# Storing one head's last rows through GpSimd in 17 small DMAs

## The chip, the cores and the metric

The kernel runs on one core of a Trainium2 chip. The core has a matrix engine (TensorE, in the profile PE, its weight loads PEld), VectorE (DVE), ScalarE (ACT), GpSimd (POOL) and SyncE (SP, which here only issues DMAs), and 16 DMA engines that move data between HBM and the on-chip memory SBUF. The results of TensorE land in PSUM and have to be copied to SBUF before a DMA can take them. The metric is the device time of one execution in microseconds (us). Before the change it is 1063.38 us, the median of 3 runs (1062.9 to 1063.62).

## The reference

For each of 8 x 12 = 96 heads, q and k are 1024 x 64 matrices in float32, and the output is the 1024 x 1024 matrix of their dot products:

```python
def reference(q, k):                      # q, k: (8, 12, 1024, 64) float32
    return np.einsum('bhid,bhjd->bhij', q, k).astype(np.float32)
```

The inputs are 50.3 MB together, the output is 402.7 MB: 4 MB (4096 KB) for each head.

## The kernel before

The 96 heads are worked off in blocks of 2, 2, 4, 8, 8 and then six times 12 heads (`sizes`). For each block, q and k are loaded in float32, cast to fp16 by GpSimd (`cast_rows`, `cast_quads`), and transposed, by TensorE for the two small blocks at the start and by VectorE for the others (`transpose_rows`, `transpose_quads`), so that the 64 elements of a row lie along partitions. Loads, casts and transposes of a later block run beside the scores of the present one. GpSimd's last cast ends long before the kernel does; after it GpSimd has nothing to do.

`scores(n, ...)` computes one head. Its output tile `o_sb` is 128 partitions x 8 rows x 1024 floats: partition p holds the output rows 8p to 8p+7, 32 KB in all, which lie side by side in HBM too. The head goes in four pieces (`u`), each of two rows of each partition: four matmuls into a PSUM tile (L171), then one copy PSUM to SBUF by ScalarE (L181), 128 x 2048 floats. After the fourth copy SP issues one DMA (L185) that stores the whole 4096 KB of the head. There are 96 such stores, all in SP's queue. SP waits before each for ScalarE's last copy of that head.

`out_pool` has three buffers, so ScalarE's first copy of head n waits until the store of head n-3 has landed. The program ends when the last store, that of head 95, has landed (SP waits for it at L304) and all engines have met in a barrier.

Instructions are issued in the order in which the source writes them (`pin` is `tc.keep_in_program_order`). The head that the change is about is `BH - 2`, number 94 counted from 0, the last but one. Its buffer isn't used again, since only head 95 comes after it, which takes the buffer of head 92.

Of the kernel before, what the change touches and what calls it, by code (L numbers as in the profile page):

```python
# [10 lines left out]
P = 128  # L11

@with_exitstack
def kernel(
# [6 lines left out]
    nc = tc.nc  # L21

    B, H, S, D = q.shape
    NT = S // P
    BH = B * H
# [5 lines left out]
    of = out.rearrange("b h i j -> (b h) i j")  # L31
# [4 lines left out]
    NMAX = max(sizes)  # L36
    CHUNK = 48 * 32

    consts = ctx.enter_context(tc.tile_pool(name="consts", bufs=1))
    ident = consts.tile([P, P], F16)  # L40

# [3 lines left out]
    out_pool = ctx.enter_context(tc.tile_pool(name="out_pool", bufs=3))  # L45

    pin = tc.keep_in_program_order

    def half_tile():
        half_sb = half_pool.tile([P, CHUNK], F16, tag="half")  # L50
        return half_sb

    class Block:
# [102 lines left out]
        def scores(self, n, side, ps_pool, w):  # L156

            half, g = divmod(n, self.N // 2)
            cs = slice(half * D, (half + 1) * D)

            qT = self.qT.rearrange("c (g m t) -> c g t m", t=NT, m=P)
            kT = self.kT.rearrange("c (g j) -> c g j", j=S)
            o_sb = out_pool.tile([P, NT, S], F32, tag="out")
            for u in range(NT // w):
                ps = ps_pool.tile([P, w * S], F32, tag="po")
                for tt in range(w):
                    for j in range(2):
                        js = slice(j * 512, (j + 1) * 512)
                        at = tt * S + j * 512
                        pin(  # L170
                            nc.tensor.matmul(  # L171
                                ps[:, at : at + 512],
                                qT[cs, g, w * u + tt],
                                kT[cs, g, js],
                            )
                        )
                dst = o_sb[:, w * u : w * u + w].rearrange("p t j -> p (t j)")
                if w == 1 and u % 2:
                    pin(nc.vector.tensor_copy(out=dst, in_=ps))  # L179
                else:  # L180
                    pin(nc.scalar.copy(out=dst, in_=ps))  # L181
                for do in side.get(u, []):
                    do()
            pin(
                nc.sync.dma_start(  # L185
                    out=of[self.first + n].rearrange("(p t) j -> p (t j)", p=P),
                    in_=o_sb.rearrange("p t j -> p (t j)"),
                )
            )

    blocks, first = [], 0
    for i, N in enumerate(sizes):
# [116 lines left out]
```

## Time and profile before

| | |
|---|---|
| median of 3 runs | 1063.38 us (1062.9 to 1063.62) |
| profiled execution: span from the first to the last instruction, the only time that its page gives | 1061.8 us |
| median less that span | 1.6 us |
| DMA traffic | 453.25 MB, mean 427 GB/s |
| busy share of PE / ACT / DVE / POOL | 66% / 66% / 44% / 35% |
| SP's stores | 96 of 4096 KB, median 21.8 us from issue to landing |
| last two stores issued by SP | about 1030.0 and 1039.4 us |
| GpSimd's last cast ends | 832.1 us |

The profile page gives the busy share of each engine, of the 16 DMA engines together, and the rate at which they move bytes, in 40 slices of the span. Views of the trace give the same for any stretch, the waits of each engine by what ended them, and the chain of work that ended last. In the view of stretches, a DMA packet (one partition's run of bytes) is counted in the stretch in which it starts, so a share over short stretches can exceed 1 or fall to 0 while an engine is still at work on one packet.

### The profile page before, as it was taken

What the parts mean: (1) busy time and instruction counts of PE and PEld (TensorE: products, weight loads), DVE (VectorE), ACT (ScalarE), POOL (GpSimd) and SP (SyncE); (2) the same over time, 40 slices, a digit from 0 to 9 for tenths busy, and PEclk for the clock granted to TensorE, in tenths of its full rate; (3) what the DMA queues carried; (4) which work ended last, traced back from release to release, by engine and by line L of the source; (5) the groups of instructions that cost most, each with busy time, mean ns of one, the idle gap of its engine ahead of it and who ended that gap; (6) DMA issues with size and microseconds to landing.
All of it is one profiled execution on the core that took longest, in us unless ns stands there. A gap on an engine that the chain in (4) does not pass through costs nothing.

```text
span 1061.8 us, 4282 instructions
## 1 busy us (share of the span) xinstructions
PE 701.3 (66%) x1568; PEld 241.6 (23%) x1568; DVE 471.5 (44%) x75; ACT 697.6 (66%) x386; POOL 368.3 (35%) x286
## 2 busy tenths in 40 slices
PE   6866755755677367773677836777367777778770
PEld 2322211211222122221222212222122222222220
DVE  2999601991696007960079600795007950000000
ACT  4856745755777366774677746777467777777771
POOL 6959128607630463303733046330463200000000
DMA  9999999999999999999999999999999999999997
GB/s 385 428 429 435 433 431 435 435 422 440 428 430 432 432 430 432 435 422 429 431 433 431 415 436 431 433 435 422 428 434 435 434 432 432 434 433 427 434 431 311
DMA packets 17588, 453.25 MB, mean 427 GB/s; under 512 B 1952, under 2 KB 1952, under 8 KB 2976
## 3 DMA queue, kind: packets, MB, share of 16 engines
q1 hardware_dynamic: 14688, 406.85, 89.1%
q10 hardware_dynamic: 2880, 46.14, 10.4%
q8 instruction: 12, 0.20, 0.1%
q14 instruction: 8, 0.07, 0.0%
HBM read 50.33 MB, written 402.65 MB: 427 GB/s over the span
## 4 chain that ended last, share of the span: by engine, by line
DMA 70%; ACT 17%; PE 7%; DVE 2%; issue 1%; POOL 1%; ACTq 0%; SPq 0%
DMA out_dram<-o_sb 70%; ACT o_sb L181 17%; PE ps L171 7%; DVE qT L145 1%; DVE kT L145 1%; DMA early<-in_q_dram 0%; POOL half_sb L127 0%; PE ps L151 0%; POOL half_sb L97 0%; DVE kT L154 0%; DVE o_sb L179 0%; ACTq L181 0%; ACT kT L154 0%; SPq L84 0%; ACTq L73 0%
## 5 line engine op out<-in xcount | busy, mean ns | idle before, releaser
L181 ACT COPY o_sb<-ps 128x2048 f32<-128x2048 f32 (+1 forms) x384 | 695.3, 1860 | 334.7 <-DMA out_dram<-o_sb 298.4
L171 PE MATMUL ps<-kT,qT 64*128 64x512 f16 x1536 | 697.2, 617 | 329.4 <-ACT o_sb L181 325.6
L127 POOL CAST half_sb<-x_sb 32x1536 f16<-32x1536 f32 (+1 forms) x256 | 346.5, 1353 | 455.1 <-DMA x_sb<-in_q_dram 318.3
L171 PEld LDWEIGHTS <-qT 64*128 64x128 f16 x1536 | 238.4, 157 | 786.3 <-issue 781.9
L145 DVE STREAM_TRANSPOSE qT<-half_sb 128x1536 f16<-128x1536 f16 (+1 forms) x34 | 232.8, 7140 | 372.2 <-issue 372.2
L145 DVE STREAM_TRANSPOSE kT<-half_sb 128x1536 f16<-128x1536 f16 (+1 forms) x34 | 234.2, 7181 | 0.0
L127 POOL CAST half_sb<-early 32x1024 f16<-32x1024 f32 x16 | 16.5, 1033 | 4.0 <-DMA early<-in_q_dram 3.3
L151 PE MATMUL ps<-ident,half_sb 128*128 128x128 f16 x32 | 4.1, 309 | 6.7 <-POOL half_sb L97 6.1
L154 DVE COPY qT<-ps 128x1024 f16<-128x1024 f16 x2 | 2.4, 1224 | 12.3 <-PE ps L151 12.3
L179 DVE COPY o_sb<-ps 128x1024 f32<-128x1024 f32 x4 | 4.9, 1224 | 4.3 <-PE ps L171 4.3
L97 POOL CAST half_sb<-early 128x512 f16<-128x512 f32 x8 | 4.6, 613 | 4.1 <-DMA early<-in_q_dram 4.1
L151 PEld LDWEIGHTS <-half_sb 128*128 128x128 f16 x32 | 3.2, 139 | 8.6 <-POOL half_sb L97 6.5
L154 ACT ACT_TABLE_LOAD x1 | 1.3, 1283 | 5.8 <-DMA early<-in_q_dram 5.8
L154 DVE COPY kT<-ps 128x1024 f16<-128x1024 f16 x1 | 1.2, 1224 | 4.3 <-PE ps L151 4.3
L154 ACT COPY kT<-ps 128x1024 f16<-128x1024 f16 x1 | 1.0, 1012 | 1.2 <-PE ps L151 1.2
masks.py:199 POOL TENSOR_SCALAR_AFFINE_SELECT ident<-ident 128x128 f16<-128x128 f16 x1 | 0.3, 292 | 0.1
masks.py:197 POOL MEMSET ident<- 128x128 f16 x1 | 0.2, 204 | 0.3 <-POOLq L293 0.3
L293 POOL MEMSET const-float32-0.0<- 128x1 f32 x1 | 0.1, 98 | 0.2 <-issue 0.2
L293 POOL MEMSET const-uint8-127<- 128x1 uint8 x1 | 0.1, 101 | 0.0
L293 POOL MEMSET const-bfloat16-1.0<- 128x1 bf16 x1 | 0.1, 100 | 0.0
L293 POOL MEMSET const-float32-1.0<- 128x1 f32 x1 | 0.1, 98 | 0.0
## 6 DMA issues: line engine op xcount, KB each, us to landing
out_dram<-o_sb SPq DMA_DIRECT2D x96, 4096.0 KB, 21.8
x_sb<-in_q_dram ACTq DMA_DIRECT2D x6, 3072.0 KB, 22.8
x_sb<-in_k_dram ACTq DMA_DIRECT2D x6, 3072.0 KB, 39.6
x_sb<-in_k_dram ACTq DMA_DIRECT2D x2, 2048.0 KB, 22.2
x_sb<-in_q_dram SPq DMA_DIRECT2D x1, 2048.0 KB, 18.0
x_sb<-in_q_dram ACTq DMA_DIRECT2D x1, 2048.0 KB, 19.0
early<-in_k_dram ACTq DMA_DIRECT2D x4, 256.0 KB, 5.0
early<-in_q_dram SPq DMA_DIRECT2D x4, 256.0 KB, 4.7
```

The costliest lines, as they stand in the source:

```text
L97: nc.gpsimd.tensor_copy(out=self.rows[x][:, :, half], in_=self.raw[x][:, half * n : (half + 1) * n].rearrange("p (r d) -> p r d", d=D),)
L127: nc.gpsimd.tensor_copy(out=half_sb[q0 : q0 + 32].rearrange("p (r d) -> p r d", d=32), in_=raw[32 * b : 32 * b + 32, c * m : (c + 1) * m, h],)
L145: pin(nc.vector.transpose(out=dst, in_=src))
L151: pin(nc.tensor.transpose(t_ps[:, t], self.rows[x][:, t], ident))
L154: pin(copy(out=dst, in_=src))
L171: nc.tensor.matmul(ps[:, at : at + 512], qT[cs, g, w * u + tt], kT[cs, g, js],)
L179: pin(nc.vector.tensor_copy(out=dst, in_=ps))
L181: pin(nc.scalar.copy(out=dst, in_=ps))
L293: nc = _bacc.Bacc("TRN2", target_bir_lowering=False, num_devices=1)
```

## The change

For head 94 alone, SP's store covers rows 0 to 6 of each partition (128 partitions x 28 KB). The eighth row of each partition, 128 x 4 KB, is stored by 17 DMAs that GpSimd issues. Each of them takes partitions that lie 9 apart: the nine diagonals 0, 9, 18, ... ; 1, 10, 19, ... ; ... are cut into chains of 15; 1 and 14; 2 and 12; 3 and 11; 4 and 10; 5 and 9; 6 and 8; 7 and 7; 13 and 1 partitions. All other heads are stored as before, by SP.

In the compiled program SP has the same number of DMAs, 96 stores, of which one is 128 x 7168 floats in place of 128 x 8192. GpSimd has 17 DMA instructions after its last cast. The first waits for ScalarE's last copy of head 94. GpSimd's DMAs have eight completion semaphores in turn, so the ninth to the seventeenth each wait, on GpSimd's queue, for the landing of the one eight before. The two chains of one partition are written as 16 pieces of 64 floats. No instruction of PE, ACT or DVE changes.

```diff
+    CHAINS = []
+    cuts = [(15,), (1, 14), (2, 12), (3, 11), (4, 10), (5, 9), (6, 8), (7, 7), (13, 1)]
+    for a, cut in enumerate(cuts):
+        for count in cut:
+            CHAINS.append((a, count))
+            a += 9 * count
...
+    def store(eng, dst, src):
+        pin(
+            eng.dma_start(
+                out=dst.rearrange("p t j -> p (t j)"),
+                in_=src.rearrange("p t j -> p (t j)"),
+            )
+        )
+
+    def store_head(head, dst, src):
+        if head != BH - 2:
+            store(nc.sync, dst, src)
+            return
+        store(nc.sync, dst[:, : NT - 1], src[:, : NT - 1])
+        for a, count in CHAINS:
+            rows = slice(a, a + 9 * (count - 1) + 1, 9)
+            store(nc.gpsimd, dst[rows, NT - 1 :], src[rows, NT - 1 :])
...
-            pin(
-                nc.sync.dma_start(
-                    out=of[self.first + n].rearrange("(p t) j -> p (t j)", p=P),
-                    in_=o_sb.rearrange("p t j -> p (t j)"),
-                )
-            )
+            dst = of[self.first + n].rearrange("(p t) j -> p t j", p=P)
+            store_head(self.first + n, dst, o_sb)
```

## The prediction

> **What bounds the kernel now.** I read the page first, its slices and DMA parts.
>
> ```profile
> span 1061.8 us, 4282 instructions
> DMA  9999999999999999999999999999999999999997
> GB/s 385 428 429 435 433 431 435 435 422 440 428 430 432 432 430 432 435 422 429 431 433 431 415 436 431 433 435 422 428 434 435 434 432 432 434 433 427 434 431 311
> HBM read 50.33 MB, written 402.65 MB: 427 GB/s over the span
> DMA 70%; ACT 17%; PE 7%; DVE 2%; issue 1%; POOL 1%; ACTq 0%; SPq 0%
> out_dram<-o_sb SPq DMA_DIRECT2D x96, 4096.0 KB, 21.8
> ```
>
> The 16 DMA engines are busy in every slice at some 430 GB/s, and only the last slice falls off (7 tenths, 311 GB/s). So bytes set the time, and a change that moves the same bytes can act only at the end, where it sits, or by disturbing the engines. At 435 GB/s one DMA engine moves 435 / 16 = 27.2 GB/s: a partition's 32 KB takes 1.2 us, a row of 4 KB 0.15 us, a head 9.64 us.
>
> Next, the last 23 us: stretches of 10, 5 and then 1 us (time, engine busy times, TensorE clock, DMA share, GB/s), the chain of waits, and SP's wait at the end.
>
> ```profile
> 1030.00:1040.00 10.00, 5.11 (x12) 1.57 (x10) 0.00 (x0) 7.29 (x4) 0.00 (x0) 1.00 1.00 429
> 1045.00:1050.00 5.00, 0.00 (x0) 0.00 (x0) 0.00 (x0) 0.00 (x0) 0.00 (x0) 1.00 0.99 426
> 1053.00:1054.00 1.00, 0.00 (x0) 0.00 (x0) 0.00 (x0) 0.00 (x0) 0.00 (x0) 1.00 0.76 328
> 1054.00:1055.00 1.00, 0.00 (x0) 0.00 (x0) 0.00 (x0) 0.00 (x0) 0.00 (x0) 1.00 0.38 164
> 1055.00:1056.00 1.00, 0.00 (x0) 0.00 (x0) 0.00 (x0) 0.00 (x0) 0.00 (x0) 1.00 0.15 66
> 1056.00:1057.00 1.00, 0.00 (x0) 0.00 (x0) 0.00 (x0) 0.00 (x0) 0.00 (x0) 1.00 0.08 33
> 1057.00:1058.00 1.00, 0.00 (x0) 0.00 (x0) 0.00 (x0) 0.00 (x0) 0.00 (x0) 1.00 0.08 33
> 1058.00:1059.00 1.00, 0.00 (x0) 0.00 (x0) 0.00 (x0) 0.00 (x0) 0.00 (x0) 1.00 0.00 0
> 1059.00:1060.00 1.00, 0.00 (x0) 0.00 (x0) 0.00 (x0) 0.00 (x0) 0.00 (x0) 1.00 0.08 33
> ```
>
> ```profile
> 1010.02 21.76 DMA out_dram<-o_sb
> ```
>
> ```profile
> SPq L304 <- DMA out_dram<-o_sb: 21.0, 1, 21.0
> out_dram<-o_sb SPq DMA_DIRECT2D x1, 4096.0 KB, 21.5
> ```
>
> The reader is to see that the DMA engines do not stop together. 33 GB/s over 1 us is 33 KB, that is one packet of 32 KB. From 1056 us on exactly one packet starts at a time, three in all (1056, 1057, 1059), so they follow each other on one engine: 15 engines are done by about 1057, and one runs 3 x 1.2 = 3.6 us longer. The last store, issued at 1039.4 us, lands 21.5 us later, at 1060.9, and that is when the one late engine is done; SP has waited 21.0 us for it. From 1053 on, 328+164+66+33+33+33 = 657 KB start. Shared by 16 engines that would be 1.5 us, so a perfectly even end would come some 4.7 us earlier (1053 + 1.5 + one packet of 1.2 = 1055.7 against 1060.4).
>
> **The change part by part.** The sum is made against the span of the profiled execution, 1061.8 us; the median is 1.6 us above it, and I add the change to the median.
>
> (1) SP's store of head 94 shrinks by an eighth. Each engine carries 8 of the 128 partitions, so each, the late one too, loses 8 x 4 KB = 32 KB: -1.2 us. SP's issue stays one instruction (0.33 us in the view of that line), and runs of 28 KB in place of 32 KB cost nothing: loads of 24 KB runs keep the slices at 430 GB/s.
>
> (2) The 128 rows come back in GpSimd's DMAs, on the same 16 engines. On the path is only how many the late engine gets, n x 0.15 us. The trace has no DMA of fewer than 128 partitions, so n lies between 0 and 15: the sizes, one each of 2 to 15 and a second 7, add 15, 15, 14, 13 ... 1, 0 rows to the engines if each DMA is dealt from the first engine on, one row to an engine (the two single rows go out in 16 pieces, 256 bytes for each engine). The term is 0 to 2.3 us; dealt evenly, 8 rows, it is 1.2 us and eats (1) up. I take 0: no DMA has 16 rows, so dealing from the front leaves one engine without any, and I take that one for the late one. This is a choice, and the second rival prices the other.
>
> (3) 17 completions on each engine. SP's stores and ACT's loads have them too and leave the share at 1.00, so nearly nothing; at most, 17 times a 2 KB packet (0.08 us at 27.2 GB/s), 1.3 us. I take 0.2, near the lower row.
>
> (4) GpSimd's own time. Its queue is empty when the DMAs come:
>
> ```profile
> 826.15 5.97 POOL L127 CAST half_sb<-x_sb 32x1536 f16<-32x1536 f32 x4 [1.76 <-DVE qT L145]
> ```
>
> The first DMA can go at about 1030.0, when SP issues the same head's store after ScalarE's last copy. Nothing is queued behind the 17 but the end of the program, so they cost nothing while the last lands before the late engine is done. The cover is 1060.9 - 1.2 - 1030.0 = 29.7 us. The trace has no DMA issued by GpSimd. Rows near it: SP's issue 0.33 us, ACT's longest issue and GpSimd's longest cast as below, 1.26 and 1.46 us, and 3.4 us as the shortest way from an issue to landing.
>
> ```profile
> L73 ACTq DMA_DIRECT2D x_sb<-in_k_dram x1: 1258/1258/1258, 734.1 to 734.1; - x1
> L127 POOL CAST half_sb<-x_sb x32: 1457/1459/1465, 698.7 to 829.2; 32x1536 f16<-32x1536 f32 x32
> DMA to landing us min/median/max: 3.4/5.4/9.4
> ```
>
> From below: 16 x 0.33 + 3.4 = 8.7 us, hidden. At 1.26: 16 x 1.26 + 3.4 = 23.6 us, still hidden, 6 us to spare. From above, each waiting for the one before to land: 17 x 3.4 = 58 us, 28 us too long. I take 1.26, a DMA issue, and so nothing; both ends stay for the rivals.
>
> The Trainium skill, "DMA: Bandwidth & Descriptors", section "Anatomy of one DMA — SWDGE (gpsimd) path", fits every DMA issued by GpSimd with 2.0 us fixed plus its bytes. Paid one after the other, that would be an estimated 17 x 2.0 = 34 us, 4 us beyond the cover. The same section puts most of the 2 us down to the write receipt, which several DMAs can wait for at once; no run here shows which it is.
>
> (5) The added waits. DMAs 9 to 17 each wait for the landing of the one eight before. Two queues on one engine take turns by packets: of two loads issued together beside the stores,
>
> ```profile
> x_sb<-in_q_dram ACTq DMA_DIRECT2D x1, 3072.0 KB, 24.7
> x_sb<-in_k_dram ACTq DMA_DIRECT2D x1, 3072.0 KB, 41.3
> ```
>
> the second lands 16.6 us after the first, and 8 packets of 24 KB with 8 of 32 KB between them are 8 x (0.9 + 1.2) = 16.8 us. So a row of GpSimd's passes one SP packet, 1.2 us, and its completion, if that takes a turn too, another: at most 2.5 us per DMA while SP's queue is full. The ninth DMA has been landed by about 1030.0 + 1.3 + 9 x 2.5 = 1053.8, the seventeenth can go a receipt later, some 1055, and is down by 1058.5 (3.4 us), inside the cover by 1 us. Cost 0. If turns are longer, what is late next is GpSimd's tail.
>
> (6) SP's last store stands behind 1.2 us less work. It is issued at 1039.4, and head 94's store, issued at 1030.0, still has nearly its 9.64 us (8.4 after the change) to run, so the queue does not run dry. Cost 0. Head 95's copies wait for head 92 and are not touched.
>
> Sum: -1.2 + 0 + 0.2 = -1.0 us. Span 1060.8, time 1062.4 us, within 0.2% (2.1 us) of the median, about what a measurement of this kernel can tell from no change.
>
> **The rivals.** *Rows dealt evenly, or the late engine among the first:* term (2) is 1.2 to 2.3 us and term (3) 0.2 to 1.3, so +0.2 to +2.4: 1063.6 to 1065.8, likeliest 1063.7. For it: nothing in the trace says which engine is late or where a small DMA starts. Against: only that even dealing is one of many cases.
>
> The Trainium skill, same page, section "Why a DMA increments its semaphore by 16 and not by 1", says that DMAs from GpSimd on k < 16 engines take k consecutive ones from a cursor that moves on, with an exception that deals from the first engine. The cursor would give the late engine 7 or 8 of the 126 rows, and by it the estimate is this rival's +0.2, the exception giving my forecast where the late engine is the last. Its section "Latency and other measured facts" names engines 7 and 15 as the usual slow ones: of them the staircase gives 15 no row and 7 eight, and the trace here only agrees that one engine is late.
>
> *GpSimd ends last (the other side):* the mechanism is GpSimd's queue of 17 issues. It decides by 0.2% when the last lands after 1060.9 + 2.1 = 1063.0, that is, with 3.4 us for the last, from (1063.0 - 1030.0 - 3.4) / 16 = 1.85 us for one issue with its wait. At 2.1 us it ends at 1030.0 + 33.6 + 3.4 = 1067.0, +6.1: 1069.5 us. For it: no row of such an issue, nine of them wait for landings, and ACT's 1.26 us is a case of a DMA issue that takes four times SP's. Against: all issues in the trace are below 1.85.
>
> *The late engine gains more than its rows:* if its lateness vanished, it would end with the next one, -3.6: 1059.8 us, faster by 0.3%. For it: it alone is late, so whatever makes it so might not come back with another mix of packets. Against: the change takes one packet's worth from it, and it is three behind.
>
> That the change does not do what it says is not a rival: the compiled order has one SP store of 7168 floats and the 17 DMAs.
>
> **How the numbers follow.** Forecast 0.52, even or reverse dealing 0.22, GpSimd last 0.20, late engine caught up 0.06. The first two end within 0.2% but for the far end of the second (1065.5 to 1065.8), which I neglect. So faster 0.06, same 0.74, slower 0.20. The range: from 1061.5 (the forecast with -1.2 and the runs' own scatter of 0.5 below) to 1066.5, which takes in all of the second and the near third of the GpSimd case; left out are the 0.06 and some 0.13.
>
> **What would show it.** In stretches of 1 us after 1050, the one-packet tail should end 1 us earlier, at about 1059.4 for (1) and (2); a tail as long as before says the rows came back to the late engine. GpSimd's DMA issues should last below 1.85 us each and the last of them begin before 1057 (4, 5). If the chain of waits ends on a DMA that GpSimd issued, the forecast is wrong by the third case; if the slices at 430 GB/s sag before 1050, by (3).

## The result, and the profile after

The changed kernel takes 1065.45 us (median of 18 runs, 1065.05 to 1066.67) against 1063.26 us (18 runs, 1062.90 to 1064.11): ratio 1.0021, 95% interval [1.0014, 1.0028]. It is 2.2 us slower. The forecast was 1062.4 us.

The profiled executions show the same step: span 1063.7 us after, 1061.8 before (+1.8; the execution profiled before was 0.4 us above its median). Bytes, mean rate and all engines but GpSimd are as they were. From the page of the changed kernel:

```profile
span 1063.7 us, 4303 instructions
q0 software_dynamic: 544, 0.53, 0.2%
HBM read 50.33 MB, written 402.65 MB: 426 GB/s over the span
DMA 73%; ACT 17%; PE 8%; issue 1%; POOL 1%; DVE 0%; ACTq 0%; POOLq 0%; SPq 0%
L58 POOL DMA_DIRECT2D out_dram<-o_sb x17 | 8.9, 526 | 215.8 <-ACT o_sb L205 197.8
```

One of GpSimd's issues takes 0.53 us on the mean. The end in stretches of 1 us (the last figures are DMA share and GB/s):

```profile
1040.00:1045.00 5.00, 0.00 (x0) 0.00 (x0) 0.00 (x0) 0.00 (x0) 1.20 (x3) 1.00 1.02 427
1045.00:1050.00 5.00, 0.00 (x0) 0.00 (x0) 0.00 (x0) 0.00 (x0) 1.39 (x3) 1.00 1.02 425
1057.00:1058.00 1.00, 0.00 (x0) 0.00 (x0) 0.00 (x0) 0.00 (x0) 0.00 (x0) 1.00 0.19 65
1058.00:1059.00 1.00, 0.00 (x0) 0.00 (x0) 0.00 (x0) 0.00 (x0) 0.00 (x0) 1.00 0.00 0
1059.00:1060.00 1.00, 0.00 (x0) 0.00 (x0) 0.00 (x0) 0.00 (x0) 0.00 (x0) 1.00 0.09 37
1060.00:1061.00 1.00, 0.00 (x0) 0.00 (x0) 0.00 (x0) 0.00 (x0) 0.00 (x0) 1.00 0.04 16
```

The tail on one engine is still there, and it now ends with 16 KB in 1060 to 1061 us, which are rows of GpSimd's. The trace's records of single packets (they carry the queue, not the DMA engine) show that last engine (start in us, length in ns, bytes, queue):

```
1055.122  1259  32768  SP
1056.378   164   4096  GpSimd    row
1056.538  1265  32768  SP
1057.799     9      4  GpSimd    completion
1057.805  1249  32768  SP
1059.051   159   4096  GpSimd    row
1059.206  1213  32768  SP        last packet of head 95
1060.415     9      4  GpSimd    a completion
1060.421     9      4  SP        the store's completion
1060.427   160   4096  GpSimd    row, then a completion of 9 ns
1060.589   159   4096  GpSimd    row, completion
1060.751   159   4096  GpSimd    row, completion
1060.912   159   4096  GpSimd    row, completion
1061.073    18    256  GpSimd    a piece of a single row, completion until 1061.096
```

On one engine each packet starts some 4 ns (at most 15) before the one before it ends, so this engine can be followed back. One packet of GpSimd's passes between two of SP's, and there is no gap from 1030.9 us on. In all three profiled executions of the change one pattern of rows alone fits the 24 packets of SP's for heads 93 to 95 and the 34 of GpSimd's. (GpSimd's are a data packet and a completion for each of 17 DMAs. An engine without a row gets 4 bytes in its place; 17 x 32 = 544 is the count above.) In that pattern the late engine has a row from every DMA of five or more partitions and none from those of two, three and four. Dealt from the first engine on, that makes it the fifth, with 12 rows. Its time from the first packet of head 93 to its last completion, in kernels that are described below:

| kernel | rows of head 94 on it | us |
|---|---|---|
| before, tiny8 | 8, within SP's 32 KB packets | 29.1, 29.1 |
| leave_out | 0 | 27.9 |
| even8, own8 | 8, in 8 DMAs | 29.3, 29.3 |
| diag9, diag9_again | 9, in 9 DMAs | 29.5, 29.5 |
| rows9 | 9, in 17 DMAs | 29.7 |
| the change (three executions) | 12, in 17 DMAs | 30.2, 30.2, 30.2 |

Against the kernel before, the change gives it 1.1 us more: its 12 rows take 1.91 us, SP's packets for the three heads 28.28 in place of 29.17 us (-0.9), and completions and small pieces some 0.1. It isn't slower than the others: in the kernel before, the others that can be followed take 29.05 to 29.20 us for the same three heads, but the late one starts on head 93 at 1031.3 us and the next at 1027.7.

In the kernel before, the last SP packet ended at 1060.398 and its completion at 1060.404. So SP's part of the late engine, 1.2 us smaller, ends at the same time (1060.419), since rows of GpSimd's went in between, and five DMAs of GpSimd's were left over: the data end 0.7 us later, at 1061.10. (The late engine was 0.4 us ahead of the kernel before when it came to head 93, at 1030.9 against 1031.3 us; with that, the difference is the 1.1 us of the table.)

The other part comes after the data. From the data's end to the span's end it was 1061.848 - 1060.404 = 1.44 us before and is 1063.661 - 1061.096 = 2.57 us now: 1.1 us more. The view of the program's last line shows what is new, first before, then after (engine, operation, count: duration in ns min/median/max, first and last start):

```profile
L304 SPq EVENT_SEMAPHORE  x7: 17/28/21024, 1039.7 to 1061.8; - x7
L304 POOLq EVENT_SEMAPHORE_RANGE_CLEAR  x1: 96/96/96, 1061.4 to 1061.4; - x1
```

```profile
L324 SPq EVENT_SEMAPHORE  x11: 17/28/28, 1061.9 to 1063.6; - x11
L324 POOLq EVENT_SEMAPHORE_RANGE_CLEAR  x1: 140/140/140, 1063.2 to 1063.2; - x1
```

SP goes through 11 semaphore instructions in place of 7. +1.1 and +0.7 are the span's +1.8. GpSimd's issues, from the timeline of its queue:

```profile
1029.44 4.23 POOL L58 DMA_DIRECT2D out_dram<-o_sb  x8 [197.75 <-ACT o_sb L205]
1038.01 0.52 POOL L58 DMA_DIRECT2D out_dram<-o_sb  x1 [4.35 <-DMA out_dram<-o_sb]
1054.21 0.52 POOL L58 DMA_DIRECT2D out_dram<-o_sb  x1 [2.07 <-DMA out_dram<-o_sb]
1055.89 0.51 POOL L58 DMA_DIRECT2D out_dram<-o_sb  x1 [1.16 <-DMA out_dram<-o_sb]
```

Eight go at once in 4.2 us; each of the other nine (three are shown) waits for the landing of the one eight before, and the last goes at 1055.9. The chain of waits now ends on GpSimd's DMAs:

```profile
1033.15 20.78 DMA out_dram<-o_sb
1054.21 0.52 POOL out_dram L58
1055.87 0.53 POOLq L324
```

### The profile page after: what moved, and what is told of

The parts are those of the page before. It is cut to its first block, busy times and chain, and to the rows that moved or that the text cites. A ratio compares the mean times of both kernels' runs of the same rounds, so it can differ in the third digit from the quotient of the medians.

```text
span 1063.7 us, 4303 instructions
## 1 busy us (share of the span) xinstructions
PE 700.9 (66%) x1568; PEld 241.8 (23%) x1568; DVE 471.4 (44%) x75; ACT 697.2 (66%) x386; POOL 377.3 (35%) x303
## 4 chain that ended last, share of the span: by engine, by line
DMA 73%; ACT 17%; PE 8%; issue 1%; POOL 1%; DVE 0%; ACTq 0%; POOLq 0%; SPq 0%
DMA out_dram<-o_sb 72%; ACT o_sb L205 17%; PE ps L195 7%; DMA early<-in_q_dram 0%; POOL out_dram L58 0%; PE ps L175 0%; POOL half_sb L121 0%; DVE kT L178 0%; DVE o_sb L203 0%; ACTq L205 0%; ACT kT L178 0%; POOLq L324 0%; SPq L108 0%
## 5 line engine op out<-in xcount | busy, mean ns | idle before, releaser
L58 POOL DMA_DIRECT2D out_dram<-o_sb x17 | 8.9, 526 | 215.8 <-ACT o_sb L205 197.8
```

Of the source, the lines that this page charges most:

```text
L58: eng.dma_start(out=dst.rearrange("p t j -> p (t j)"), in_=src.rearrange("p t j -> p (t j)"),)
```

## The experiments

The theory after this reading: *late engine and end waits*. One engine ends late; the small DMAs are dealt from the first engine on and gave that engine more rows than it lost; and the program's end waits for eight semaphores more. The rivals: *GpSimd's tail* (issues, waits and landings of the 17 DMAs set the end), and *packets that meet* (rows dealt to other engines lengthen packets). All edits are in `store_head`, in place of the 17 DMAs; SP's store of 128 x 28 KB stays unless the diff says otherwise. Every ratio is against the kernel before on the same chip.

### Rows of head 94 left out, and dealt evenly

```diff
         store(nc.sync, dst[:, : NT - 1], src[:, : NT - 1])
-        for a, count in CHAINS:
-            ...
# leave_out: nothing; even8 (and even8_again):
+        for a in range(8):
+            rows = slice(16 * a, 16 * a + 16)
+            store(nc.gpsimd, dst[rows, NT - 1 :], src[rows, NT - 1 :])
```

leave_out: 

> The eighth rows of head 94 are not stored at all (this part of the output is missing); SP's store of 128 x 28 KB stays. Theory 'late engine': one DMA engine alone sets the end, in unprofiled runs too, and loses 8 x 4 KB, 1.2 us: 1063.26 - 1.2 = 1062.1 us, the one-packet tail as long as before but 1.2 us earlier. Rival 'GpSimd's tail': the end is set by when the small DMAs are through, and the store before was not bound by one engine: also shorter, but by no more than the 0.5 MB of all engines, 1.2 us, with the tail of single packets gone or changed. If the end hangs on something else than the bytes of an engine, no change: 1063.3.

even8: 

> The eighth rows go out by GpSimd in 8 DMAs of 16 partitions, one row for each of the 16 engines: every engine gets back the 8 rows that it lost, no DMA waits for the landing of another, and all eight completion semaphores of GpSimd are in use. Theory 'late engine and end waits': the late engine's data end as before (-1.2 + 8 x 0.159 + some completions = +0.1 to +0.2 us), and the program's end still takes some 0.8 us longer, for SP waits for eight semaphores more: 1064.1 to 1064.3 us. Rival 'GpSimd's tail' (the waits for landings and the issue at 1055.9 us cost the time): nothing left of it: 1063.3. Rival 'small packets slow all engines': as many small bytes as in the change: the landing late by the same 1.0 us, 1064.9 to 1065.4.

leave_out: 1061.92 us, ratio 0.9989 [0.9980, 0.9998], -1.3 us against 1063.24 us. Without the rows the end moves by one packet's worth, so the bytes of the late engines set the end, in unprofiled runs too. In the profiled execution (1062.93 us, the slowest of the 11) two engines were late, at 1059.3 and 1059.7 us, and the next at 1054.4.

even8: 1064.99 us, 1.0017 [1.0008, 1.0026], +1.75 us. No landing is waited for and GpSimd is through with its issues in 4 us, but the time is not back: the tail alone is not it. In the packets the late engine takes 29.3 us, 0.2 more than before, as the theory gave; the data end at 1060.36 us, as before the change, and the end of the program takes 2.45 us in place of 1.44. The profiled execution took 1064.59 us, and the median lies 0.7 us above the upper end of what the theory gave (1064.3).

### The end of the program by itself

```diff
     def store_head(head, dst, src):
-        ...
+        store(nc.sync, dst, src)
+        if head == 40:
+            for a in range(8):
+                pin(nc.gpsimd.dma_start(out=scratch[:, 16 * a : 16 * a + 16],
+                                        in_=qf[16 * a : 16 * a + 16, :16]))
```

tiny8: 

> All stores by SP as before the change; beside head 40 GpSimd issues 8 DMAs of 16 partitions x 64 bytes into a scratch tile that nobody reads, one for each of its eight completion semaphores, 600 us before the end. Theory 'end waits': only that GpSimd's eight semaphores are in use at all costs 0.85 us at the program's end, where SP waits for each in turn: 1064.1 us, with SP's four more semaphore waits seen at the end of the span. Rival: the time after the last landing grew because those DMAs had only just landed: then nothing is left, 1063.3.

1064.60 us, 1.0013 [1.0004, 1.0022], +1.3 us. All stores are SP's; eight DMAs of 1 KB, over 600 us before, and the kernel is slower. The data end at 1060.37 us as before (1060.40), and the rest takes 2.43 us in place of 1.44, +1.0 us. SP's semaphores at the end:

```profile
L327 SPq EVENT_SEMAPHORE  x11: 17/28/28, 1039.7 to 1062.7; - x11
SPq L327 <- DMA out_dram<-o_sb: 21.1, 2, 11.5
```

Eleven again, where the last store itself landed after the same wait (21.1 us in all, 21.0 before). The trace's record of the instructions shows that all waits but the first are for two semaphores each. Before, five instructions pass nine semaphores, and two of the five come after the landing of the last store; in tiny8 nine pass seventeen, and six come after it; in the change eight of nine come after the last landing:

| us | data's end to SP's seeing it | SP's waits after that | barrier to the span's end |
|---|---|---|---|
| before | 0.48 | 0.20 | 0.76 |
| tiny8 | 0.51 | 0.79 | 1.13 |
| the change | 0.80 | 0.94 | 0.83 |

So SP's waits themselves cost 0.6 and 0.7 us more than before. Some 0.35 of that is one pause between two instructions, and neither that pause nor the longer barrier of tiny8 is explained by the record. One GpSimd semaphore (one128, below) costs 0.1 us: 1.55 us after the data. In the other kernels with eight GpSimd semaphores the part after the data is 2.2 to 2.6 us, and 2.0 in two of them (mid and few4, below).

### One GpSimd DMA, and the diagonals uncut

```diff
# one128:
+        store(nc.gpsimd, dst[:, NT - 1 :], src[:, NT - 1 :])
# diag9 (and diag9_again):
+        for a in range(9):
+            store(nc.gpsimd, dst[a::9, NT - 1 :], src[a::9, NT - 1 :])
```

one128: 

> The eighth rows of head 94 go out in a single GpSimd DMA of 128 partitions, 8 rows to an engine. Theory 'late engine, end waits, and small packets that last longer where they meet': one semaphore more, 0.1 us; rows of 0.159 us (seen where they do not meet) give -1.2 + 1.3 = +0.1, rows of 0.27 us (mean with 16 neighbouring partitions in flight) give -1.2 + 2.1 = +0.9: 1063.4 to 1064.3 us. Rival 'GpSimd as such slows the engines': as slow as the change, 1065.4.

diag9: 

> The nine diagonals uncut: 9 GpSimd DMAs of 15 and 14 partitions, which dealt from the first engine give 9 rows to each of the engines 1 to 14, 2 to the fifteenth, none to the last. Theory 'late engine' (12 rows of the change went to it, if it is the fifth): 3 rows fewer, -1.2 + 9 x 0.159 to 0.19 = +0.2 to +0.5, and the end waits of 0.85: 1064.3 to 1064.6 us. Rival 'GpSimd's tail': one DMA alone waits for a landing, all are through by 1045: 1064.1 with the end waits.

one128: 1063.65 us, 1.0003 [0.9994, 1.0012]: no difference that the runs can tell. Its 128 rows take 159 ns each, and SP's 32 KB packets after 1031 us 1.220 us on the mean (1.216 before the change). So GpSimd as such slows nothing that the runs can tell: its queue and 0.5 MB are free when one DMA carries them.

diag9: 1064.67 us, 1.0013 [1.0005, 1.0022], +1.4 us, of which the end is 1.1 (2.51 against 1.44 us). Rows take 203 ns, 32 KB packets 1.233 us. The data end as before the change, at 1060.40 us; the engine that ends last there is another, 0.05 us after the usual one.

### The change on an earlier head

```diff
-        if head != BH - 2:
+        if head != BH - 10:
```

mid: 

> The change itself, made on head 86 (ninth from the end of the 96 heads, 80 us before the end) in place of head 94; head 94 is stored whole. Theory 'late engine': that engine never idles, so its rows cost the same wherever they are put, and the end waits stay: 1065.2 to 1065.5 us, as with the change. Rival 'GpSimd's tail': the small DMAs left over after SP's last store of the late engine (0.7 us at the end of the changed kernel) and their landing are what is late; put elsewhere, only the end waits stay: 1064.1.

1075.56 us, 1.0116 [1.0102, 1.0130], +12.3 us, which neither theory had. The buffer of head 86 is used again by head 89, and ScalarE's first copy into it has to wait for all 17 DMAs. Three views of this kernel, the chain, the waits and stretches:

```profile
951.00 3.71 POOL out_dram L58 x7
954.71 20.47 DMA out_dram<-o_sb
976.99 16.11 DMA out_dram<-o_sb
```

```profile
ACT o_sb L205 <- DMA out_dram<-o_sb: 43.2, 10, 22.4
```

```profile
970.00:980.00 10.00, 2.78 (x7) 0.91 (x6) 0.00 (x0) 0.87 (x1) 1.99 (x4) 1.00 1.00 416
980.00:990.00 10.00, 0.00 (x0) 0.00 (x0) 0.00 (x0) 0.00 (x0) 0.00 (x0) 1.00 0.76 315
990.00:1000.00 10.00, 4.65 (x11) 1.56 (x11) 0.00 (x0) 6.57 (x4) 0.00 (x0) 1.00 0.01 4
```

From the first issue at 951.0 to the last landing at 993.1 it takes 42 us, 2.5 us per DMA, where SP's store of the same head took 21.4. ScalarE waits up to 22.4 us and the DMA engines stand still for most of 10 us. So the chain of 17 DMAs is slow, and in the changed kernel it is hidden only because head 94's buffer isn't used again. As a test of the late engine the run fails: another wait covers what it was to show.

### Which engine is late: rows dealt by SP

```diff
# sp119, sp125, sp116, sp92: n = 119, 125, 116, 92
+        for rows in (slice(0, n), slice(n, P)):
+            store(nc.sync, dst[rows, NT - 1 :], src[rows, NT - 1 :])
```

sp119: 

> No GpSimd. The eighth rows go out by SP in two DMAs, of 119 partitions (7 x 17, dealt to 7 engines if the number of engines is the largest divisor up to 16) and of 9. Theory 'late engine', with the rows dealt from the first engine on and the late one among the first seven: it gets 17 or 18 rows of 0.15 us, -1.2 + 2.7 = +1.5 us: 1064.8 us, and no longer end of the program than one or two waits of 0.08 us. If the late engine is not among the first seven, it gets none or one: 1062.1. Rivals 'GpSimd's tail' and 'small packets from GpSimd': nothing of GpSimd is left, 1063.3.

sp125: 

> No GpSimd. The eighth rows go out by SP in two DMAs, of 125 partitions (5 engines, 25 rows each) and of 3. The packets of the changed kernel gave the late engine rows in the DMAs of 8, 7, 7 and 13 partitions and 10 or 11 rows in all, which makes it the sixth or seventh. Theory 'late engine': then it gets no row, and loses 1.2 us; the first five get 4 us more but were done 6 us earlier: 1062.1 us. If it is among the first five: -1.2 + 25 x 0.159 = +2.8, 1066.0. Rivals: 1063.3.

sp116: 

> No GpSimd. The eighth rows go out by SP in DMAs of 116 partitions (4 x 29) and 12: the first four engines get 29 rows and one, the next eight one. 125 partitions on five engines were 5.1 us slower than before, so the late engine is one of the first five. Theory 'late engine', if it is the fifth: 1 row, -1.2 + 0.2 = -1.0 us, but the first four now end as late (30 rows of 0.16 to 0.22 us, less the 1.2 us: +3.6 to +5.4 on engines that were done 6 us earlier): 1062.3 to 1063.0 us. If it is one of the first four: -1.2 + 30 x 0.2 = +4.8 or more, 1068 to 1069.

sp92: 

> As the one before, with 92 partitions (4 x 23) and 36 (12 x 3): the fifth engine gets 3 rows in place of 8, the first four 26. If the fifth is the late one: -1.2 + 0.5 to 0.65 + 0.1 to 0.2 for two semaphores more = -0.4 to -0.6 us, 1062.6 to 1062.9 us, with the first four done in time. If it is one of the first four: -1.2 + 26 x 0.2 = +4, 1067.

| | median, us | ratio, interval | against before | data end, profile |
|---|---|---|---|---|
| sp119 (7 engines x 17) | 1066.53 | 1.0031 [1.0019, 1.0042] | +3.3 | 1063.56 |
| sp125 (5 x 25) | 1068.32 | 1.0046 [1.0034, 1.0059] | +5.1 | 1065.32 |
| sp116 (4 x 29) | 1066.35 (1063.5 to 1068.2) | 1.0026 [1.0016, 1.0035] | +3.1 | 1064.55 |
| sp92 (4 x 23) | 1064.62 (1063.1 to 1067.6) | 1.0017 [1.0007, 1.0027] | +1.3 | 1059.51 |

sp119 and sp125 use no GpSimd and are slower than before, sp125 more; this is the late engine again, and none of GpSimd's. The packets of sp125's last engine show rows in a row until 1055.63 us, 22 of which can be followed back to 1050.08 (0.25 us each), then eight packets of SP's until 1065.32, so it is one of the five that get 25 rows. (The expectation took the change's late engine for the sixth or seventh; followed back packet by packet it is the fifth.) sp119 and sp125 are 1.7 and 2.3 us beyond what rows of 0.159 us give; 0.5 of that is the end (1.9 us after the data), and their rows took 0.22 and 0.26 us on the mean.

sp116 was to be faster than before and is 3.1 us slower. In its profiled execution, the slowest of the nine, the last engine has 30 rows, from 1047.6 to 1054.9 us, where rows on other engines run from 1042.5 to 1050.2. So in that execution the engine that was behind is one of the first four that SP's DMA is dealt to, and not the fifth. Whether SP's and GpSimd's DMAs count the engines alike isn't shown. On the chip of sp116 and sp92 single runs lie 4.5 us apart, so one fixed late engine does not explain those two, and why they scatter stays open.

### Fewer rows in more DMAs, and the same number of DMAs with other rows

```diff
# few4:
+        for a in range(8):
+            n = 16 if a % 2 else 4
+            for b in range(0, 16, n):
+                rows = slice(a + 8 * b, a + 8 * (b + n - 1) + 1, 8)
+                store(nc.gpsimd, dst[rows, NT - 1 :], src[rows, NT - 1 :])
# rows9, the 17 chains cut otherwise:
-    cuts = [(15,), (1, 14), (2, 12), (3, 11), (4, 10), (5, 9), (6, 8), (7, 7), (13, 1)]
+    cuts = [(15,), (11, 4)] + [(10, 4)] * 7
```

few4: 

> 20 GpSimd DMAs in place of 17: 16 of 4 partitions and 4 of 16, so about as many waits for landings and issues as in the change (12 in place of 9), and the same end waits. Dealt from the first engine on, the first four engines get 20 rows, all others 4. Theory 'late engine', if it is the fifth: 4 rows in place of 12, 8 x 0.16 = 1.3 us less than the change: -1.2 + 0.65 + 1.0 to 1.1 for the end = 1063.7 to 1064.1 us. If it is one of the first four: 20 rows, 1066.5 or more. Rival 'GpSimd's tail': a longer chain of small DMAs, so no shorter than the change: 1065.4 to 1066.5. Rival 'dealt in turn from a cursor': 8 rows for each engine, 1064.4 to 1064.9.

rows9: 

> 17 GpSimd DMAs as in the change, over the same diagonals, cut otherwise: 15; 11 and 4; seven times 10 and 4 partitions. Dealt from the first engine, the fifth gets 9 rows (12 in the change), the first four 17 (12 to 15 plus the two split rows). Theory 'the rows on the late engine count', if it is the fifth: 3 rows of 0.16 to 0.2 us fewer than the change: 0.5 to 0.6 us faster than the change beside it, 1064.9 us. If it is one of the first four: 2 to 5 rows more, 1065.8 to 1066.5. Rival 'the number of DMAs and their waits count': as the change, 1065.5.

diag9_again: 

> The nine uncut diagonals once more, on the same chip as the one above: 9 rows for the late engine (the fifth), 9 DMAs in place of 17, one wait for a landing in place of nine: 1064.7 us by its first run. Theory 'rows': 0 to 0.3 us faster than the 17 DMAs with 9 rows. Rival 'number of DMAs': 0.8 us faster than those.

change_third: 

> The change itself on the same chip, for the two above: 1065.3 to 1065.7 us.

few4: 1066.76 us, 1.0035 [1.0023, 1.0047], +3.5 us. With 20 DMAs GpSimd's chain does end last. SP's last packet is done at 1060.03 us (its completion at 1060.18), and GpSimd has still to issue; its queue and the stretches:

```profile
1059.19 0.52 POOL L58 DMA_DIRECT2D out_dram<-o_sb  x1 [2.06 <-DMA out_dram<-o_sb]
1060.98 1.02 POOL L58 DMA_DIRECT2D out_dram<-o_sb  x2 [1.27 <-DMA out_dram<-o_sb]
```

```profile
1059.00:1060.00 1.00, 0.00 (x0) 0.00 (x0) 0.00 (x0) 0.00 (x0) 0.52 (x1) 1.00 0.02 4
1061.00:1062.00 1.00, 0.00 (x0) 0.00 (x0) 0.00 (x0) 0.00 (x0) 1.00 (x2) 1.00 0.01 4
1062.00:1063.00 1.00, 0.00 (x0) 0.00 (x0) 0.00 (x0) 0.00 (x0) 0.01 (x1) 1.00 0.27 82
```

The engines stand idle for it, and the data end at 1062.99. In the changed kernel no such gap is seen: its late engine goes from packet to packet to the end.

On one chip: rows9 1065.79 us (1.0023 [1.0014, 1.0032]), change_third 1065.40 (1.0021 [1.0012, 1.0030]), diag9_again 1065.08 (1.0013 [1.0005, 1.0022]), before 1063.37. rows9 is not 0.5 us faster than the change but 0.4 slower, the time that was expected for a late engine among the first four, which have 17 rows there. The packets show why, and it is another reason: two engines end late. The usual late one has rows from the DMAs of 10, 11 and 15 partitions alone, 9 in all, and is through at 1060.60 us; its three heads take 29.70 us, 0.52 less than in the change, which is the 0.5 us of the expectation. The engine that ends last, at 1062.03, has six rows from six DMAs in succession after its last SP packet, though these are of 10 and 4 partitions in turn: only the first four engines get a row of each. Its last SP packet took 1.90 us in place of 1.21. So the three rows count as expected on the engine that was late, and the rows dealt to the first four made one of those later still. The time of rows9 by itself does not exclude the rival (the change and rows9 have 17 DMAs and overlap), and diag9_again lies nearer to the change here (0.3 us) than diag9's first run did.

### Packets that meet

```diff
# own8, against even8_again:
-            rows = slice(16 * a, 16 * a + 16)
-            store(nc.gpsimd, dst[rows, NT - 1 :], src[rows, NT - 1 :])
+            store(nc.gpsimd, dst[a::8, NT - 1 :], src[a::8, NT - 1 :])
```

own8: 

> As the 8 GpSimd DMAs of 16 partitions before (8 rows for each engine, eight semaphores, no waits for landings), but each takes partitions 8 apart in place of 16 neighbours. Theory 'packets that meet': SP's stores give each DMA engine 8 neighbouring partitions, and a row read by another engine than its partition's own meets that engine's packets; partitions 8 apart put every row on its own engine: rows of 0.16 us (0.27 with neighbours), 32 KB packets after 1031 us of 1.22 us (1.26), and the data end as before the change; with the end waits of 1.0 us: 1064.3 to 1064.6 us. Rival 'only the rows on the late engine count': no difference to the neighbours' kernel, 1065.0.

even8_again: 

> The 8 GpSimd DMAs of 16 neighbouring partitions once more, beside the one above on the same chip: 1065.0 us, rows of 0.27 us and 32 KB packets of 1.26 us on the mean. Under the rival the same time as the one above.

change_again: 

> The change itself, on the same chip as the two above: 1065.2 to 1065.7 us. If the late engine's place differs from chip to chip, its time differs from 1065.45, between 1063.5 (a late engine without rows: -1.2 + 0.2 + 1.1 for the end, and the meetings) and 1066.5 (15 rows).

own8 1064.42 us (1.0014 [1.0005, 1.0023]), even8_again 1064.71 (1.0015 [1.0006, 1.0024]), change_again 1065.55 (1.0023 [1.0014, 1.0032]), before 1063.14. own8 lies where the theory put it, but not for its reason: its rows take 204 ns (240 in even8_again) and its 32 KB packets 1.259 us (1.254), so what it took for granted, that SP's stores give an engine 8 neighbouring partitions and that partitions 8 apart put each row on its own engine, isn't borne out. On the usual late engine own8 and even8 do not differ, 29.3 us each. What the packets do show, over all kernels on the mean of all engines: rows take 159 ns and 32 KB packets 1.220 us where one DMA of 128 partitions carries them (one128), 194 to 266 ns and 1.233 to 1.275 us where they go out in DMAs of fewer partitions, by GpSimd or by SP. That rows in such DMAs go with longer packets is shown; why is not, and that packets meet is only argued. The late engine has little of it: its rows take 0.16 to 0.17 us in the change. The change gave the same time on every chip it ran on, 1065.40 to 1065.55 us.

No kernel here that stores all rows beats the kernel before.

## Why the prediction was wrong

**What bounds the kernel:** right. The last engines' bytes set the end; leave_out, -1.3 us, measures the packet that the forecast wanted to gain (step 1, -1.2; the late engine takes 27.9 us there in place of 29.1). In the change SP's packets on the late engine gain 0.9 of it, for some of them got longer.

**Step (2) failed.** It took 0 for the rows that the late engine gets back, as a choice: dealing from the first engine leaves one engine without rows, and that one was taken for the late one. Dealing from the first engine is borne out: the late engine takes a row from each of five DMAs in succession, those of 6, 8, 7, 7 and 13 partitions by the order of issue, and 6 + 8 + 7 + 7 engines dealt in turn would pass each of 16 engines at most twice. But the engine without rows isn't the late one. The late one is the fifth in the order of dealing and gets 12 rows, 1.91 us where the forecast had 0. Three rows fewer with the same 17 DMAs (rows9) bring that engine to its end 0.52 us sooner. Staircase and place are what the prediction's second rival had, +0.2 to +2.4 us and at most 1065.8; measured it is -0.9 + 1.9 + 0.1 = +1.1. The median's part that is not the end is 2.2 - 1.1 = 1.1. Of the rules of the Trainium skill ("DMA: Bandwidth & Descriptors") that the prediction weighed, the exception that deals from the first engine agrees with these packets and the moving cursor, which would give 7 or 8 rows, does not; the engines 7 and 15 of "Latency and other measured facts", to which that dealing gives 8 rows and none, are not the late ones here.

**A term was missing:** 1.1 us at the program's end, 1.0 in tiny8, for the eight completion semaphores that GpSimd's DMAs bring into use. The prediction counted each DMA's completion on the engines (step 3) and the waits on GpSimd's queue (step 5), but not that SP waits for each semaphore at the end, after the last byte, where nothing hides it. tiny8 shows it alone. In part it was to be seen: SP's seven semaphore instructions on the program's last line were in the trace before. This term carries the change over the 0.2%; with it, the second rival is the result. That 1065.45 us lies in the stated range, and below that rival's 1065.8, is in part luck, since half of the 2.2 us comes from the end, which none of the cases counted.

**Step (3)**, 0.2 us for completions, was nearly right in size: completions are 9 ns each, and with the small pieces some 0.1 us on the late engine. What it left out is that packets beside the rows get longer (32 KB packets 1.258 us against 1.216 on the mean of all engines), 0.3 us in all on the late engine, the part of step (1) that wasn't gained.

**Step (4)** took 1.26 us for an issue of GpSimd's; it is 0.53. The cover held, as said. **Step (5)** was right: the two queues take turns by packets (the list above), 2.5 us per DMA, the seventeenth issued at some 1055; measured 42 / 17 = 2.5 in mid, and 1055.9. **Step (6)** held: the DMA share is 1.02 between 1040 and 1050.

**The rivals.** GpSimd ending last did not decide the change, though its rows are the last data. The sign that the prediction gave for it, a chain of waits that ends on a DMA of GpSimd's, did come, but it doesn't tell the cases apart: the last rows stood behind SP's packets on the late engine, which went from packet to packet without a gap, so no wait of GpSimd's held it up. With 20 DMAs (few4) GpSimd does end last, 3.0 us after SP's last packet, not through the length of an issue, on which the prediction put it, but through the waits for landings. The late engine caught up: no.

## What to carry to other kernels

Count what a new queue costs at the program's end: each completion semaphore that comes into use is waited for after the last byte, and here eight cost 0.6 to 1.1 us, 1.0 where their DMAs had long landed (tiny8). Small DMAs beside a full queue of large packets get through one packet at a time, so a row of them holds its buffer for long; put them only where that buffer isn't needed soon. Before rows are moved to unload a late engine, find out which engine is late and where small DMAs are dealt: twelve rows on the late one cost more (1.9 us) than it was relieved of (1.2 us).

## What was not expected of the hardware

Seventeen DMAs of 0.5 MB together took 42 us to land beside a busy queue and cost 12.3 us where a buffer waited for them (mid). The engine that ends late isn't alone in every execution: 15 engines ended by 1056.7 us in the kernel before, but in leave_out two were late by 5 us. In the kernel before it works no slower than the others over the last three heads; it comes to them 3.6 us late, and what makes it late before that was not tried. Rows dealt by SP to four engines scattered by 4.5 us from run to run on one chip (sp92, sp116), which stays open.
